# A two-layer decoder trunk on one core: which pairs of the second up projection run as seven products, and the order of work around them

## The chip, the core and the metric

One core of one Trainium2 chip. The metric is the device time of one execution in microseconds (us), median of several runs. The kernel before takes 1085.06 us (three runs, 1084.51 to 1085.06).

## The reference, cut to what matters

```python
def short_conv_mixer(h, w_in, conv_w, w_out):
    b_gate, c_gate, u = jnp.split(h @ w_in, 3, axis=-1)
    v = c_gate * u
    ...
    return (b_gate * conv) @ w_out

def squared_relu_mlp(h, w1, w2):
    return jnp.square(jax.nn.relu(h @ w1)) @ w2

def reference(x, ...):
    for layer in range(DEPTH):                       # 2 layers
        h = rms_norm(x, norm_mix[layer])
        if layer < N_A_LAYERS:                       # layer 0
            x = x + short_conv_mixer(h, ...)
        else:                                        # layer 1
            x = x + nsa_mixer(h, ..., shared, rel_bias)
        x = x + squared_relu_mlp(rms_norm(x, norm_mlp[layer]), mlp_w1[layer], mlp_w2[layer])
        if layer == N_A_LAYERS - 1:
            shared = nsa_shared_kv(rms_norm(x, kv_norm), w_kv, ...)
    return rms_norm(x, final_norm)
```

512 tokens, model width 1024, hidden width 4096, everything in float32.

## The kernel before, in words

**Arithmetic.** Each float32 operand is split into a high and a low float16 half (`whi`, `wlo` for a weight; `xs`, `rh` and `rl` for activations), and a product of two takes three matmuls: high by high, low by high, high by low. The halves of the weights are made on the chip: DMA brings a float32 piece (`wst`), ScalarE (ACT) writes the high half, VectorE (DVE) the low one. `next_piece` hands pieces out in a fixed list, `ahead` converts some pieces ahead of use.

**Seven products.** Many of the large products are done block-wise with seven products of half-size blocks in place of eight. The price is sums of blocks, of the weights (`W_SUMS`, four additions on VectorE for each half piece) and of the activations (`R_SUMS`), and a combination of the results.

**An MLP.** The hidden width is done in two halves. A half is an up projection (`mlp_up`: eight pairs of 128 hidden channels, p = 0 to 7) and a down projection (`mlp_down`: four pairs of output channels, always as seven products, summing over eight hidden chunks c = 0 to 7 into the seven halves of banks "aabb" or "ccde"). A plain pair of an up projection is 48 matmuls of 512 columns in two accumulators from `acc()`; a pair as seven products (`seven`, only in the second up projection, for the pairs in `UP7`) is 84 matmuls of 256 columns. For these, the block sums of x are computed during the first up projection, kept in DRAM (`kept`), and loaded back by two DMAs that GpSimd (POOL) issues, into the parts 5 to 7 of the hidden activations `rh` and `rl`: these parts must first have been read for the last time by the down projection. For the pairs in `MADE7` the sums and splits of the weights are done earlier in the kernel and kept in DRAM (`make_seven`), so that at use there are only loads.

**Stages, from the start:** the short convolution mixer of layer 0 with its output projection (four pairs), the MLP of layer 0 (up, down, up, down), the attention of layer 1 with its output projection, the MLP of layer 1, the final norm.

**What sets the order.** Accumulators of plain pairs turn through "aabbcc" (`acc`; the counter `turn[0]` is set to 1 at each up projection and otherwise runs on). The first mixer, the second up projection of each layer and the attention are each recorded as a plan: a list scheduler (`Plan.issue`) orders the recorded instructions of all engines by keys, and the tables in `SHIFTS`, one per plan, shift the keys of single instructions (before, only the fourth, for the second up projection of layer 1, has entries). What is outside a plan is ordered by the framework. In the profile a line 268 is an instruction of a plan, a line 302 one outside; after the change these lines are 342 and 376.

Of the kernel before, what the change touches and what calls it, by code (L numbers as in the profile page):

```python
# [10 lines left out]
F32 = mybir.dt.float32  # L11
# [27 lines left out]
def onehot_buckets():  # L39
# [5 lines left out]


SHIFTS = (
    (),
    (),
    (),  # L50
    (
# [15 lines left out]
    ),  # L67
)

# [238 lines left out]
def body(ctx, tc, x, rel_bias, norm_mix, norm_mlp, mlp_w1, mlp_w2, a_w_in, a_conv_w, a_w_out,  # L308
# [26 lines left out]
    def begin_plan(**late):  # L335
        banks.clear()
        turns.clear()
        plan.begin(*[u for i in sorted(ready) for u in ready[i]], *[staged[i] for i in sorted(staged)], **late)
# [23 lines left out]
    def seven_blocks(w, c0):  # L362
        v = w.rearrange("(c j p) n -> c p j n", j=2, p=128)
        for c in (0, 2):
            pieces.append(([v[c + k, :, :, c0:c0 + 256] for k in range(2)], None, SW))

    def down_blocks(w, p, half):

        v = w.rearrange("(j c p) n -> c p j n", j=2, p=128)
        for c in range(8 * half, 8 * half + 8, 2):  # L370
            pieces.append(([v[c + k, :, :, p * 256:(p + 1) * 256] for k in range(2)], None, SW2))

    def mlp_pieces(layer):
# [12 lines left out]


    SEVEN = [(2, 1), (2, 0), (3, 1), (3, 2), (3, 0)]
    UP7 = ((2, 3, 5), (1, 2, 3, 5))
    MADE7 = ((), (1,))  # L390
    FILL_AT, FILL = 4, 1
    made, made_out = {}, {}
    v = a_w_in[0].rearrange("(c p) (s n) -> c p s n", p=128, s=3)
# [385 lines left out]
        ACT.activation(dst[0], z[:, 4:8], AF.Copy)  # L779
        DVE.tensor_tensor(dst[1], z[:, 4:8], dst[0], op=OP.subtract)  # L780

    def seven(xs, sums, names, dlo, dhi=None):
        X_, W_, V_ = (bank(g)[:, 0:256] for g in "abc")
        ws = [next_piece(), next_piece()]
        cv = ahead()

        def block_of(hl, c, b):
            if b < 4:
                return xs[hl][:, 2 * c + b // 2, (b % 2) * 256:(b % 2) * 256 + 256]
            return sums[hl][:, 4 * c + b - 4]  # L790

        def product(i, ps, more=False):
            a, b = PRODUCTS[i]
            for c in range(4):
                wh, wl = (u[:, c % 2, a - 1] for u in ws[c // 2])
                xh, xl = (block_of(hl, c, b) for hl in range(2))
                PE.matmul(ps, wh, xh, start=c == 0 and not more, stop=False, skip_group_check=more)
                PE.matmul(ps, wl, xh, start=False, stop=False, skip_group_check=more)
                PE.matmul(ps, wh, xl, start=False, stop=c == 3, skip_group_check=more)

        u2, u5 = (wk[0].tile([128, 256], F32, name=n, bufs=1) for n in names)
        product(0, X_)
        ACT.activation(W_, X_, AF.Copy)
        product(4, V_)
        ACT.activation(u5, V_, AF.Copy)
        next(cv, None)
        product(2, W_, True)
        ACT.activation(u2, W_, AF.Copy)
        product(5, V_, True)
        DVE.tensor_tensor(dlo[:, 1], V_, u2, op=OP.add)  # L810
        next(cv, None)
        product(3, W_, True)
        DVE.tensor_tensor(dlo[:, 0], W_, u5, op=OP.add)
        product(1, X_, True)
        if dhi is not None:
            ACT.activation(dhi[:, 1], X_, AF.Copy)
        drain(cv)
        product(6, W_, True)
        if dhi is not None:
            ACT.activation(dhi[:, 0], W_, AF.Copy)  # L820
        return dlo, W_, X_
# [114 lines left out]
    for p in range(4):  # L936
        po = [acc(), acc()]
        pair(ys, po)
        if p < 3:
            drain(ahead())  # L940
        split_some(PACE_OUT[p])
        for m in range(2):
            residual_in(po[m], 2 * p + m, 1.0 / (SY * SW))
            ss.add(X[:, 2 * p + m])
        for m in range(2):
            split_gain(xs, 2 * p + m, X[:, 2 * p + m], "mlp0")
        drain(ahead())
# [8 lines left out]
    def mlp_up(xs, ss, rh, half, rb, gname, kept):  # L956
        turn[0], layer = 1, int(gname[-1])
        first = half == 0
        if not first:
            sums = [u[:, 5:8].rearrange("p a b n -> p (a b) n")[:, 0:16] for u in rh]  # L960
            for hl in range(2):
                POOL.dma_start(sums[hl], kept[:, hl])

        def rows():
            nonlocal rb
# [23 lines left out]
        for p in range(8):  # L989
            if not first and p in UP7[layer]:  # L990
                dlo = wk[0].tile([128, 2, 256], F32, name="dn_w", bufs=1)
                held[p] = seven(xs, sums, ("dn_p", "sv_u"), dlo)
                drain(ahead())
                squares(p)
                continue
            held[p] = [acc(), acc()]
            pair(xs, held[p], mid={ROOT_AT: ss.rstd} if first and p == 0 else {ROWS_AT: rows} if first and p == 1 else {})
            drain(ahead())
            if p or not first:
                squares(p)  # L1000
            if first and p in SUMS_AT:
                c = SUMS_AT.index(p)
                z = wk[0].tile([128, 8, 256], F32, name="ml_z", bufs=2)
                block_sums(c, gname, z, [u[:, 7, 0:4] for u in rh])
                for hl in range(2):
                    SPQ.dma_start(kept[:, hl, 4 * c:4 * c + 4], rh[hl][:, 7, 0:4])
# [34 lines left out]
    def mlp_down(rh, done, mid=None, last=None):  # L1041

        post = iter(())
        for p in range(4):
            bk = [bank(g) for g in ("aabb" if p % 2 == 0 else "ccde")]
            late = last and p == 3
            slot = {0: 0, 2: 2, 3: 4, 4: 6, 5: 1} if late else range(7)
# [3 lines left out]
            def product(i, c, w, terms=(0, 1, 2)):  # L1051

                a, b = PRODUCTS[i]
                wh, wl = (u[:, a - 1] for u in w)
                xh, xl = (u[:, c, b - 1] for u in rh)
                other = i == 5 if late else i % 2 == 1
                for n in terms:
                    PE.matmul(acc7[i], wl if n == 1 else wh, xl if n == 2 else xh, stop=c == 7 and n == 2,
                              start=c == 0 and n == 0 and not other, skip_group_check=other)

            some = (0, 2, 3, 4, 5) if late else range(7)
            ws = []
            for c in range(0, 4 if late else 8, 2):
                w = next_piece()
                for k in range(2):
                    for terms in ((0, 1), (2,)) if p == 0 and c + k == 7 else ((0, 1, 2),):
                        for i in some:
                            product(i, c + k, [u[:, k] for u in w], terms)
                    ws.append([u[:, k] for u in w])
                    behind = None  # L1070
                    if c + k == 0 and p:
                        behind = copied[0]
                    if c + k == 5 and mid and p:
                        behind = mid(p)
                    if k == (1 if c == 4 and mid else 0):
                        with tc.issue_after(behind.ins) if behind else nullcontext():
                            drain(ahead())
                    if c + k or not p:
                        next(post, None)
# [10 lines left out]
    def first_half(hp, xs, ss, gname):  # L1090
# [1 line left out]
        rh = tuple(hp.tile([128, 8, 7, 256], F16, name=n) for n in ("rh", "rl"))  # L1092
        rb = mlp_up(xs, ss, rh, 0, None, gname, kept)
        mlp_down(rh, None)
        begin_plan(DVE=3500.0, ACT=1000.0)
        mlp_up(xs, ss, rh, 1, rb, gname, kept)
        plan.issue()
        return rh
# [606 lines left out]
    xs = xm  # L1705
# [167 lines left out]
```

## Time and profile before

| | us |
|---|---|
| median of three runs | 1085.06 |
| the profiled execution | 1084.73 |
| its span, first to last instruction | 1082.9 |
| first mixer | 0 to 172.3 |
| layer 0: up, down, up, down | to 256.4, 329.8, 409.1, 482 |
| attention with output projection | to 763.5 |
| layer 1: up, down, up, down and final norm | to 847.6, 921, 999.1, 1082.9 |

The profile gives for each engine the busy time, and for each instruction its start, its length, and what ended the idle time before it. A start and a length in one row may stand for several equal instructions (x2, x7). Matmuls overlap, so their rate is read from one start to the next, not from the length of one. "PE" is TensorE; PEclk is its granted clock, 1.00 for 2.4 GHz.

### The profile page before, as it was taken

What the parts mean: (1) busy time and instruction counts of PE and PEld (TensorE: products, weight loads), DVE (VectorE), ACT (ScalarE), POOL (GpSimd) and SP (SyncE); (2) the same over time, 40 slices, a digit from 0 to 9 for tenths busy, and PEclk for the clock granted to TensorE, in tenths of its full rate; (3) what the DMA queues carried; (4) which work ended last, traced back from release to release, by engine and by line L of the source; (5) the groups of instructions that cost most, each with busy time, mean ns of one, the idle gap of its engine ahead of it and who ended that gap; (6) DMA issues with size and microseconds to landing.
All of it is one profiled execution on the core that took longest, in us unless ns stands there. A gap on an engine that the chain in (4) does not pass through costs nothing.

```text
span 1082.9 us, 21537 instructions
## 1 busy us (share of the span) xinstructions
PE 1072.7 (99%) x8442; PEld 737.6 (68%) x8442; DVE 953.3 (88%) x1824; ACT 619.8 (57%) x1010; POOL 64.9 (6%) x93
## 2 busy tenths in 40 slices
PE   9999999999999999999999999999999999999997
PEld 4457844446885768886766696675444788775897
DVE  7999987998985999989886789997899796899996
ACT  6665555666333654437766687865666532464453
POOL 2000000000000000000002022311000000000022
PEclk9999999999999999999999999999999999999999
DMA  8535788453432334306634262002753236521332
GB/s 278 170 105 176 233 270 254 149 162 126 129 112 103 115 119 137 100 20 178 198 111 124 78 196 80 21 21 60 215 155 125 71 117 188 173 79 59 104 113 79
DMA packets 160774, 143.48 MB, mean 133 GB/s; under 512 B 9388, under 2 KB 149376, under 8 KB 160160
## 3 DMA queue, kind: packets, MB, share of 16 engines
q1 hardware_dynamic: 157248, 132.61, 39.8%
q10 hardware_dynamic: 2464, 4.70, 1.4%
q0 software_dynamic: 960, 4.80, 1.2%
q8 instruction: 66, 1.08, 0.4%
q14 instruction: 36, 0.29, 0.1%
HBM read 123.55 MB, written 15.51 MB: 128 GB/s over the span
## 4 chain that ended last, share of the span: by engine, by line
PE 94%; DVE 3%; ACT 1%; issue 1%; POOL 0%; POOLq 0%; ACTq 0%; DVEq 0%
PE a L268 19%; PE b L268 16%; PE c L268 14%; PE c L302 13%; PE a L302 12%; PE b L302 12%; PE d L302 4%; PE d L268 3%; PE e L302 2%; DVE at_s L268 1%; PE e L268 1%; ACT xq L268 0%; DVE wlo L268 0%; DVE X L302 0%; DVE wst L268 0%
## 5 line engine op out<-in xcount | busy, mean ns | idle before, releaser
L302 PEld LDWEIGHTS <-whi 128*128 128x128 f16 x2272 | 222.3, 98 | 79.8
L268 PEld LDWEIGHTS <-whi 128*128 128x128 f16 x1824 | 175.6, 98 | 114.7 <-issue 1.6
L302 ACT ACTIVATE whi<-wst 128x1792 f16<-128x1792 f32 (+1 forms) x92 | 132.8, 1458 | 111.5 <-DVE wst L302 53.5
L302 DVE SCALAR_TENSOR_TENSOR wlo<-wst,whi 128x1792 f16<-128x1792 f32 (+1 forms) x92 | 158.0, 1724 | 5.3 <-ACT whi L302 5.3
L268 ACT ACTIVATE whi<-wst 128x896 f16<-128x896 f32 (+5 forms) x144 | 116.5, 843 | 70.3 <-DVE wst L268 19.1
L268 DVE SCALAR_TENSOR_TENSOR wlo<-wst,whi 128x896 f16<-128x896 f32 (+5 forms) x144 | 135.1, 964 | 9.9 <-ACT whi L268 9.6
L302 PEld LDWEIGHTS <-wlo 128*128 128x128 f16 x1136 | 111.1, 98 | 40.6
L268 PEld LDWEIGHTS <-wlo 128*128 128x128 f16 x912 | 89.2, 98 | 64.8 <-DVE wlo L268 0.9
L302 DVE TENSOR_TENSOR wst<-wst 128x256 f32<-128x256 f32 x232 | 89.5, 430 | 11.5 <-DMA wst<-mlp_w_dram 10.5
L268 ACT ACTIVATE at_p<-at_s,at_m 128x128 f32<-128x128 f32 (+3 forms) x128 | 71.0, 556 | 29.2 <-DVE at_m L268 26.8
L268 PE MATMUL a<-xs,whi 128*128 128x512 f16 (+2 forms) x368 | 85.6, 321 | 0.1
L268 DVE CUSTOM_DVE_ANT_0 at_s<-b,T 128x128 f32<-128x128 f32 (+3 forms) x128 | 59.2, 486 | 15.6 <-PE b L268 13.5
L302 PE MATMUL a<-rh,whi 128*128 128x256 f16 x256 | 69.1, 273 | 0.0
L302 PE MATMUL a<-rh,wlo 128*128 128x256 f16 x256 | 69.1, 273 | 0.0
L302 PE MATMUL a<-rl,whi 128*128 128x256 f16 x256 | 67.8, 273 | 0.0
L302 PE MATMUL c<-rh,whi 128*128 128x256 f16 x248 | 67.6, 273 | 0.0
L302 PE MATMUL c<-rh,wlo 128*128 128x256 f16 x248 | 67.6, 273 | 0.0
L302 PE MATMUL c<-rl,whi 128*128 128x256 f16 x248 | 67.6, 273 | 0.0
L268 ACT ACTIVATE at_ph<-c 128x512 f16<-128x512 f32 (+2 forms) x96 | 51.0, 533 | 20.2 <-PE c L268 17.7
L268 DVE SCALAR_TENSOR_TENSOR at_pl<-c,at_ph 128x512 f16<-128x512 f32 (+2 forms) x96 | 59.2, 618 | 2.5 <-ACT at_ph L268 2.2
L268 PE MATMUL b<-xs,whi 128*128 128x512 f16 (+1 forms) x248 | 60.2, 327 | 0.0
L268 PE MATMUL a<-xs,wlo 128*128 128x512 f16 (+2 forms) x184 | 58.4, 321 | 0.0
(314 smaller groups left out, 2490.6 us busy)
## 6 DMA issues: line engine op xcount, KB each, us to landing
wst<-mlp_w_dram SPq DMA_DIRECT2D x228, 256.0 KB, 3.6
early<-pre_hl SPq DMA_DIRECT2D x14, 512.0 KB, 3.6
wst<-mlp_w_dram SPq DMA_DIRECT2D x48, 128.0 KB, 2.7
wst<-a_w_in_dram SPq DMA_DIRECT2D x20, 256.0 KB, 3.8
wst<-w_kv_dram SPq DMA_DIRECT2D x10, 512.0 KB, 4.5
T<-ext_d ACTq DMA_DIRECT2D x4, 1056.0 KB, 5.8
wst<-a_w_in_dram SPq DMA_DIRECT2D x8, 512.0 KB, 4.7
wst<-a_w_out_dram SPq DMA_DIRECT2D x8, 512.0 KB, 4.0
```

The lines of the kernel that those rows point to most:

```text
L268: getattr(self.engines[t["e"]], t["op"])(*t["args"], **t["kw"])
L302: return real(*args, **kwargs)
```

## The change

- `UP7`: pair 0 of the second up projection becomes seven products in both layers; in layer 1 pair 1 becomes a plain pair. `seven` gets the banks for pair 0 as "aba" in place of "abc".
- `MADE7`: pair 2 of both layers has its sums and splits made early. In layer 0 that happens at the last pair of the first mixer's output projection, in layer 1 in the attention stage as before (there for pair 1).
- `LAST_FIRST`: the last pair of each first down projection reads the hidden chunks 4 to 7 first, then 0 to 3. The loads of x's block sums are issued ahead of the plan of the up projection.
- `SHIFTS`: tables for the first mixer (372 entries) and for both second up projections (one table of 115 entries for both, in place of the one of layer 1).

```diff
 SHIFTS = (
-    (),
-    (),
+    (
+        (8, -10837), (9, -9292.8), (10, -8766.4), (11, -8651.3), (12, -7709.2), (13, -8454.9), (14, -3982.6),
...
+    ),
+    (
+        (24, -791.7), (27, -2324), (50, 2128.2), (53, -278.2), (56, 1133.3), (58, 944.9), (59, 309.9), (61, -167),
...
+    ),
     (),
...
+    LAST_FIRST = ((0, 2, 4, 6), (4, 6, 0, 2))
+
     def down_blocks(w, p, half):
 
         v = w.rearrange("(j c p) n -> c p j n", j=2, p=128)
-        for c in range(8 * half, 8 * half + 8, 2):
+        for c in (8 * half + u for u in LAST_FIRST[not half and p == 3]):
...
-    UP7 = ((2, 3, 5), (1, 2, 3, 5))
-    MADE7 = ((), (1,))
+    UP7 = ((0, 2, 3, 5), (0, 2, 3, 5))
+    MADE7 = ((2,), (2,))
...
-    def seven(xs, sums, names, dlo, dhi=None):
-        X_, W_, V_ = (bank(g)[:, 0:256] for g in "abc")
+    def seven(xs, sums, names, dlo, dhi=None, groups="abc"):
+        X_, W_, V_ = (bank(g)[:, 0:256] for g in groups)
...
         split_some(PACE_OUT[p])
+        for j in MADE7[0] if p == 3 else ():
+            now = []
+
+            def raw_half():
+                now[:] = [wk[0].tile([128, PIECE], F32, name="pre_in", bufs=2)]
+                return now[0][:, 0:512]
+            drain(make_seven(0, j, raw_half, lambda: now[0][:, 512:PIECE], lambda: wk[0].tile(
+                [128, 2, PIECE], F16, name="pre_hl", bufs=2)[:, :, 0:896].rearrange("p i (b n) -> p i b n", n=128)))
...
-        if not first:
-            sums = [u[:, 5:8].rearrange("p a b n -> p (a b) n")[:, 0:16] for u in rh]
-            for hl in range(2):
-                POOL.dma_start(sums[hl], kept[:, hl])
+        sums = [u[:, 5:8].rearrange("p a b n -> p (a b) n")[:, 0:16] for u in rh]
...
-                held[p] = seven(xs, sums, ("dn_p", "sv_u"), dlo)
+                held[p] = seven(xs, sums, ("dn_p", "sv_u"), dlo, groups="abc" if p else "aba")
...
+            at = LAST_FIRST[done is None and p == 3]
...
-                    PE.matmul(acc7[i], wl if n == 1 else wh, xl if n == 2 else xh, stop=c == 7 and n == 2,
-                              start=c == 0 and n == 0 and not other, skip_group_check=other)
+                    PE.matmul(acc7[i], wl if n == 1 else wh, xl if n == 2 else xh, stop=c == at[3] + 1 and n == 2,
+                              start=c == at[0] and n == 0 and not other, skip_group_check=other)
...
-                            product(i, c + k, [u[:, k] for u in w], terms)
+                            product(i, at[c // 2] + k, [u[:, k] for u in w], terms)
...
-        begin_plan(DVE=3500.0, ACT=1000.0)
+        soon = 0 in UP7[int(gname[-1])]
+
+        def load_sums():
+            for hl in range(2):
+                POOL.dma_start(rh[hl][:, 5:8].rearrange("p a b n -> p (a b) n")[:, 0:16], kept[:, hl])
+        if soon:
+            load_sums()
+        begin_plan(DVE=7000.0 if soon else 3500.0, ACT=1000.0)
+        if not soon:
+            load_sums()
```

What this does to the order of instructions is shown at three places.

VectorE between the third and the last pair of the first down projection of layer 0 (`wst` are weights, summed in place; `X<-c` is the combination of the last pair). Before:

```order
L302 TENSOR_TENSOR X<-X,dn_w 128x2x256
L268 TENSOR_TENSOR wst_3322<-wst_3322 128x2x128 x4
L268 TENSOR_TENSOR wst_3327<-wst_3327 128x2x128 x3
L268 SCALAR_TENSOR_TENSOR wlo_3427<-wst_3322,whi_3426 128x896 x2
L302 SCALAR_TENSOR_TENSOR X<-c,X 128x256
```

Now:

```order
L376 TENSOR_TENSOR X<-X,dn_w 128x2x256
L376 TENSOR_TENSOR wst_3159<-wst_3159 128x2x128 x3
L376 TENSOR_TENSOR wst_3214<-wst_3214 128x2x128
L376 TENSOR_TENSOR wst_3159<-wst_3159 128x2x128
L376 TENSOR_TENSOR wst_3214<-wst_3214 128x2x128 x3
L342 TENSOR_TENSOR wst_3284<-wst_3284 128x2x128
L376 SCALAR_TENSOR_TENSOR wlo_3385<-wst_3159,whi_3384 128x1792
L376 SCALAR_TENSOR_TENSOR wlo_3443<-wst_3214,whi_3442 128x1792
L376 SCALAR_TENSOR_TENSOR X<-c,X 128x256
```

The sums and splits of pair 0's two pieces stand ahead of the end of the down projection, where before work of pair 2 stood.

VectorE at the lead-in of the attention (`KD` and `Q` are the first keys and queries, `rb` the row factors). Before:

```order
L268 TENSOR_TENSOR at_s_5164<-a,rb 128x512
L268 TENSOR_TENSOR at_s_5165<-a,rb 128x512
L268 SCALAR_TENSOR_TENSOR xq<-X,vec,xq 128x512
L268 TENSOR_TENSOR KD<-at_s_5164,KD 64x512 x2
...
L268 TENSOR_TENSOR at_s_5175<-b,rb 128x512
L268 TENSOR_TENSOR at_s_5164<-b,rb 128x512
L268 TENSOR_TENSOR sq<-sq,ssacc 128x128
L268 TENSOR_TENSOR Q_5174<-at_s_5175,Q_5174 64x512 x2
```

Now:

```order
L342 TENSOR_TENSOR at_s_5252<-c,rb 128x512
L342 TENSOR_TENSOR at_s_5253<-c,rb 128x512
L342 SCALAR_TENSOR_TENSOR xq<-X,vec,xq 128x512
L342 TENSOR_TENSOR KD<-at_s_5252,KD 64x512 x2
...
L342 TENSOR_TENSOR at_s_5263<-a,rb 128x512
L342 TENSOR_TENSOR at_s_5252<-a,rb 128x512
L342 TENSOR_TENSOR sq<-sq,ssacc 128x128
L342 TENSOR_TENSOR Q_5262<-at_s_5263,Q_5262 64x512 x2
```

The keys lie in bank c in place of a, the queries in a in place of b; the values that TensorE does after the queries are in a both times.

TensorE where the output projection of the attention (`big`) goes over into the first up projection of layer 1 (`xs`). Before:

```order
L268 MATMUL c<-big,whi 128x512
L268 LDWEIGHTS wlo
L268 MATMUL c<-big,wlo 128x512
L302 LDWEIGHTS whi
L302 MATMUL b<-xs,whi 128x512
```

Now:

```order
L342 MATMUL b_5275<-big_5326,wlo_5412 128x512
L376 LDWEIGHTS whi_9409
L376 MATMUL c_9456<-xs_5406,whi_9409 128x512
...
L376 MATMUL c_9457<-xs_5406,wlo_9410 128x512
L376 LDWEIGHTS whi_5417
L376 MATMUL b_9383<-xs_5406,whi_5417 128x512
```

The last output pair lies in bank b in place of c, and 12 matmuls of pair 1 (bank c) stand ahead of pair 0 (bank b).

## Rows read from the trace of the kernel before

**Rows 1.** Page, busy time, share of the span and instructions of TensorE:

```profile
PE 1072.7 (99%) x8442; PEld 737.6 (68%) x8442; DVE 953.3 (88%) x1824; ACT 619.8 (57%) x1010; POOL 64.9 (6%) x93
```

**Rows 2.** Busy time by stretch; the first line names the columns:

```profile
core 0: us, PE busy (x) PEld busy (x) DVE busy (x) ACT busy (x) POOL busy (x), PEclk, DMA share, GB/s
0.00:172.30 172.30, 170.92 (x1001) 99.03 (x1002) 154.68 (x248) 103.34 (x156) 5.86 (x13) 1.00 0.67 211
256.40:329.80 73.40, 73.40 (x674) 65.73 (x672) 60.64 (x99) 27.14 (x21) 0.00 (x0) 1.00 0.38 115
329.80:409.10 79.30, 79.30 (x495) 48.14 (x493) 71.28 (x119) 42.58 (x47) 1.14 (x2) 1.00 0.38 120
921.00:999.10 78.10, 78.10 (x530) 51.65 (x529) 72.36 (x120) 41.07 (x46) 1.06 (x2) 1.00 0.34 106
640.00:720.00 80.00, 77.91 (x952) 58.58 (x948) 76.54 (x234) 62.24 (x173) 18.69 (x26) 1.00 0.21 65
1062.00:1082.90 20.90, 14.64 (x180) 13.72 (x178) 11.61 (x29) 5.67 (x22) 5.77 (x8) 0.90 0.26 101
```

**Rows 3.** Timeline of POOL from 328; then the page's DMA issues (median to landing):

```profile
329.92 0.61 POOL L268 DMA_DIRECT2D rh<-kept_mlp  x1 [146.46 <-PE e L302]
330.55 0.53 POOL L268 DMA_DIRECT2D rl<-kept_mlp  x1
...
rh<-kept_mlp POOLq DMA_DIRECT2D x2, 1024.0 KB, 6.2
```

**Rows 4.** Timeline of DVE, 316 to 329 (start, length, idle before and its end):

```profile
316.36 2.68 DVE L268 TENSOR_TENSOR wst<-wst 128x256 f32<-128x256 f32 x7
319.05 2.09 DVE L268 SCALAR_TENSOR_TENSOR wlo<-wst,whi 128x896 f16<-128x896 f32 x2
328.68 0.42 DVE L302 SCALAR_TENSOR_TENSOR X<-c,X 128x256 f32<-128x256 f32 x1 [7.53 <-ACT dn_p L302]
```

**Rows 5.** Timelines of DVE, POOL and PE, 161 to 185:

```profile
161.35 0.69 DVE L268 SCALAR_TENSOR_TENSOR X<-a,X 128x512 f32<-128x512 f32 x1 [1.30 <-PE a L268]
...
169.35 1.23 DVE L268 SCALAR_TENSOR_TENSOR pre_hl<-pre_in,pre_hl 128x1024 f16<-128x1024 f32 x1 [1.44 <-ACT pre_hl L268]
...
178.41 1.22 DVE L302 SCALAR_TENSOR_TENSOR wlo<-wst,whi 128x1024 f16<-128x1024 f32 x1 [1.43 <-ACT whi L302]
182.21 0.16 DVE L302 TENSOR_SCALAR rs_a<-d 128x4 f32<-128x4 f32 x1 [2.57 <-PE d L302]
...
182.45 1.02 POOL L302 TENSOR_TENSOR rs_r<-rs_a,expo 128x4 f32<-128x4 f32 x1 [158.84 <-DVE rs_a L302]
...
184.62 0.60 PE L302 MATMUL e<-ident,rs_r 128*128 128x128 f32 x4
```

**Rows 6.** Timelines of DVE and PE at the attention's lead-in, 504 to 507:

```profile
504.32 0.28 DVE L268 TENSOR_TENSOR sq<-ssacc 128x128 f32<-128x128 f32 x1
504.52 1.28 DVE L268 TENSOR_TENSOR at_s<-b,rb 128x512 f32<-128x512 f32 x2
...
504.27 0.27 PE L268 MATMUL a<-whi,xs 128*128 128x256 f16 x1
...
506.77 0.29 PE L268 MATMUL b<-KD,Q 128*128 128x128 f16 x2 [0.37 <-DVE Q L268]
```

**Rows 7.** Timelines of DVE and PE where layer 1's first up projection begins:

```profile
763.02 1.22 DVE L302 SCALAR_TENSOR_TENSOR wlo<-wst,whi 128x1024 f16<-128x1024 f32 x1
...
766.02 1.28 DVE L268 SCALAR_TENSOR_TENSOR X<-c,X 128x512 f32<-128x512 f32 x2
...
763.74 0.38 PE L302 MATMUL b<-xs,wlo 128*128 128x512 f16 x1
```

**Rows 8.** Timeline of PE, 5 to 7, filling matmuls ahead of the first real one:

```profile
5.53 1.06 PE L268 MATMUL c<-idle 128*128 128x512 f16 x2
```

**Rows 9.** Timelines of PE and POOL behind the sum of squares, 773 to 775:

```profile
773.18 0.59 PE L302 MATMUL b<-xs,whi 128*128 128x512 f16 x2
...
773.60 1.17 POOL L302 TENSOR_TENSOR rs_r<-rs_a,expo 128x4 f32<-128x4 f32 x1 [26.82 <-DMA wst<-mlp_w_dram]
```

100 rows, old and new, of the table SHIFTS are left out of this document.

## Prediction

> **What bounds the kernel now.** I read the page's busy times first, then the busy time of each engine by stage, then the timelines of single engines around the seams between stages. TensorE is busy for 1072.7 us of 1082.9 [rows 1]. The stage table says where the missing 10 us of TensorE lie [rows 2]: in the four MLP stretches it has none (73.40 of 73.40, 79.30 of 79.30, 78.10 of 78.10). Some 1.4 us are in the first stage, 2.1 in 640 to 720, 6.3 in the last 21 us. So in the stretches that the change is about, the time is the number of matmul columns and nothing else; VectorE has 8 us of air in the second up projection of layer 0 and 5.7 in that of layer 1. Two things can move the total: fewer columns, or a wait of TensorE that is not there now. The reader should see that all idle time outside the end of the kernel is under 4 us, so that no rearrangement can win much more than the columns it saves. What a measurement of this kernel tells from no change is about 0.2%, 2.2 us.
>
> **Pair 0 as seven products.** The table has the price without any model: the second up projection of layer 0 is five plain pairs and three of seven products, 79.30 us; that of layer 1 is four and four, 78.10 us [rows 2]. One pair turned over is worth 1.20 us. The change brings layer 0 to four and four, so **-1.20 us**. Layer 1 has four before and after (pair 0 takes the place of pair 1): **0**.
>
> **The reload of x's block sums.** Now both loads are issued at 329.92 and 330.55, when the up projection has begun, and land 6.2 us after issue (median) [rows 3]. Pair 0 needs them at its second product, 12 matmuls in. A matmul of the down projection (256 columns) takes 73.40 / 672 = 0.109 us, so one of 512 columns (79.30 - 3 x 84 x 0.109) / 240 = 0.216 [rows 2]; the new order frees the blocks 88 matmuls, 9.6 us, before the end instead of 4. Issued at about 320.2 and 320.8 they land near 327; they are needed at 329.8 + 12 x 0.109 = 331.1. Slack about 4 us, cost 0. POOL has nothing else queued there. What is behind the loads on POOL is not due for tens of us.
>
> **Preparing pair 0.** Its two pieces need 8 additions on VectorE (2.68 / 7 = 0.38 us each) and two splits of 1792 columns, each as long as the 2.09 us that two of 896 take [rows 4]: 7.2 us, against 7.53 us in which VectorE stands idle before the end of that down projection [rows 4], where 2.68 + 2.09 us of plan work also give way. Walking it from 316.36, with ScalarE's conversions in between, the second piece is ready near 324.5, 5 us before it is due. Cost 0; without that gap those 7 us would fall into the up projection, which has 8 us of VectorE to spare.
>
> **Pair 2's sums kept in DRAM.** In the second up projection of layer 0 pair 2's sums and splits go, 8 x 0.38 + 4 x 1.045 = 7.2 us of VectorE, replaced by loads; TensorE doesn't wait there, so nothing is gained. The same work, cut smaller, moves ahead of the last output projection of the first mixer: 16 additions of 128 columns at 0.20 us (start to start, the second of [rows 6] after the first) and 8 splits at up to 0.64 us (half of the two-instruction row of [rows 7]) are at most 8.3 us; the lower bound is the 7.2 above. VectorE has there 1.30 + 1.44 + 1.43 + 2.57 = 6.7 us of idle time [rows 5], and the new order runs the two banks of the last two output pairs one after the other, so that the first is free for VectorE 24 x 0.216 = 5.2 us sooner. What is late next, if it does not fit, is the sum of squares: rs_a at 182.21, POOL's power until 183.47, the transposes at 184.62 [rows 5], 1.15 between the last two, of which I leave 0.15 for the handover: 1.0 us of slack. Bounds 0 and 8.3 - 6.7 - 1.0 = 0.6 us; I take 0, because of the bank that comes free sooner. In layer 1 the same work only changes its pair: 0.
>
> **The start.** The new table puts the copy of the gains ahead of the first weight conversion on ScalarE. The first real matmul follows two filling ones that take 1.06 us from 5.53 [rows 8]; it can't come sooner than by these. Bounds -1.1 and, for an order that is late by half as much, +0.5; I take **-0.3**, since the split of x's first block still stands in between.
>
> **Banks.** This is what the diff does not show. Two plain pairs fewer take four turns fewer of the rotating banks, and later stages inherit it. At the lead-in of the attention the first queries now lie in bank a, and the values that follow them go to the same bank. VectorE empties the first half of the queries from 504.52 [rows 6], 0.64 us, so the values, due at 504.27, begin at about 505.2: 0.95 late. Ahead of the first logits stand 15 of them instead of 18, and the logits already waited for Q: 18 from 504.27 end at 506.23, and they start at 506.77 [rows 6]. The logits come at 505.2 + 15 x 0.109 = 506.86, 0.09 later than now and with three matmuls fewer done: **+0.4 us**.
>
> At the seam from the attention to the first up projection of layer 1 the last output pair now lies in bank b, where pair 0 wants to begin. TensorE therefore takes 12 matmuls of pair 1 first. Their low weight half is made by VectorE from 763.02, 1.22 us; it is due with the third matmul, at 763.74: +0.55. After them (12 x 0.216 = 2.6 us) pair 0 begins at 766.45 and its bank is emptied from 766.02, 0.64 each [rows 7]: +0.25. Together **+0.8 us**, between 0 (VectorE ahead by as much) and 1.5 (a split more in front).
>
> Behind that, the transposes of the row factors come right after the last chunk, which starts at 773.18 and has 6 matmuls (to 774.48), while POOL's power ends at 773.60 + 1.17 = 774.77 [rows 9]; now more chunks stand in between. **+0.3**, between 0 and 0.5.
>
> **The sum.** -1.20 - 0.3 + 0.4 + 0.8 + 0.3 = 0.0. The profiled execution took 1084.73 us (span 1082.9 and 1.8 around it), 0.33 under the median of the runs, 1085.06. So 1084.7 beside the profiled one and 1085.0 beside the median; I give 1084.9.
>
> **The rivals.**
> *The savings stay and the bank waits don't count (0.22).* The two waits are each under 1 us and come from my walk of VectorE; if VectorE is ahead by that much there, -1.2 and up to -1.1 at the start, with up to 1 us of the first stage's 1.4, remain: 1081.7 to 1083.9 beside the median, about two thirds of it past the bound of 2.2. For it: the idle time that TensorE has in 640 to 720 (77.91 of 80.00) [rows 2] could swallow a lead-in that is late. Against it: VectorE is busy 76.54 of 80.00 there, so what is late for VectorE stays late.
>
> *VectorE is late at the end of the first mixer (slower, 0.07).* If none of the four gaps can be used, since each ends with a wait of its own, 8.3 us less the 1.0 of slack come out as a wait of TensorE for the row factors: +7.3, 1092. It is slower by over 0.2% from the point at which less than 8.3 - 1.0 - 2.2 = 5.1 us of the 6.7 are usable.
>
> *The reload comes late (slower, 0.04).* POOL's issue must get through while VectorE works through pair 0's sums and splits. Here two issues took 0.61 and 0.53 us beside VectorE's additions from PSUM and SBUF [rows 3]; if each had to wait out one split of 2.09 us [rows 4], they land 4.2 us later, near 331.2, just at the need. What is over costs in both layers: it decides from 5.2 us late (2 x 1.1), and 7 us late are 2 x 2.9 = +5.8, 1090.7. The Trainium skill has a rule that speaks for it: in SBUF — State Buffer, section Who interferes with whom, a VectorE instruction in a two-port mode locks GpSimd out and so holds up the descriptors of a load issued there. The trace of this stretch has only instructions with two tensor inputs on VectorE [rows 4], and shows no such hold.
>
> *Waits lower TensorE's clock (slower, 0.02).* With waits of some 0.5 us in a row, as at the new seams, the clock could fall from 2.4 to 1.2 GHz, and 5 us of work after it would take 10: 1090. In 640 to 720, where TensorE loses 2.1 us in many small waits, the granted clock is 1.00; it is lower only at the end (0.90 from 1062 on) [rows 2]. TensorE: Matmul & The Clock Gate of the Trainium skill, section A second HAM failure mode: psum-queue depth-cycling, says that short idle times between groups that turn through the banks make the clock swing; the stretch from 640 to 720 does not agree.
>
> *The change does nothing to the count* can be excluded: the program has 48 matmuls of 512 columns less and 84 of 256 more.
>
> **How the numbers follow.** My own case, within about 1.5 us of 1084.9, has 0.65. The four rivals take 0.35; 0.08 of the first stays within the bound. The range goes from within the first rival, 1082.4, to my case with the upper bound of every term (-1.2 + 0.5 + 0.6 + 0.4 + 1.5 + 0.5 = +2.3) on the median: 1087.4. Faster by over 0.2%: 0.14, the rest of the first rival; within it 0.65 + 0.08 = 0.73; slower 0.07 + 0.04 + 0.02 = 0.13.
>
> **What would show it.** The second up projection of layer 0 in 78.1 us with TensorE busy throughout; both reloads issued about 9 us before it; TensorE's gap before the values near 504, and one near 763 before the third matmul of bank c. Wrong it would be if TensorE idles over 1 us before product 2 of pair 0, at the transposes near 184, or if the clock falls below 1.00 before 1060.

## The result, and the profile after

The changed kernel takes 1091.01 us (1090.69 to 1091.43, four runs) against 1084.88 for the kernel before beside it; the ratio is 1.0057, 95% interval 1.0042 to 1.0071. It is slower by 6.1 us, and outside the range that was given. Its profiled execution has a span of 1089.2 us.

The seams between the stages, read from the starts of TensorE's matmuls in both traces, say where the time went:

| stretch | before, us | after, us | difference |
|---|---|---|---|
| start to the first up projection | 172.16 | 172.64 | +0.48 |
| layer 0: up and down | 157.48 | 157.48 | 0 |
| layer 0: second up | 79.31 | 83.37 | +4.06 |
| layer 0: second down | 73.36 | 73.98 | +0.62 |
| attention with output projection | 281.00 | 281.09 | +0.09 |
| layer 1: first up | 84.12 | 85.16 | +1.04 |
| layer 1: down, second up, rest | 235.5 | 235.5 | 0 |

First the page's busy line of the changed kernel, which answers to [rows 1]:

```profile
PE 1073.9 (99%) x8478; PEld 741.6 (68%) x8478; DVE 955.7 (88%) x1845; ACT 622.4 (57%) x1015; POOL 62.8 (6%) x93
```

TensorE is busy 1.2 us longer although it has 1.2 us of work less; the window view (columns as in [rows 2]) shows where most of this lies: the second up projection of layer 0, where the work is less, is busy for 79.80 us in place of 79.30.

```profile
172.60:330.00 157.40, 157.40 (x1068) 104.60 (x1067) 137.62 (x225) 80.33 (x74) 2.16 (x3) 1.00 0.49 151
330.00:332.50 2.50, 0.40 (x4) 0.11 (x2) 2.22 (x2) 0.00 (x0) 0.00 (x0) 1.00 0.00 1
332.50:335.00 2.50, 1.20 (x8) 0.79 (x9) 2.50 (x4) 0.00 (x0) 0.00 (x0) 0.87 0.22 64
335.00:337.70 2.70, 2.70 (x15) 1.92 (x13) 2.70 (x8) 1.33 (x2) 0.00 (x0) 0.50 0.83 205
330.30:413.50 83.20, 79.80 (x529) 52.26 (x528) 75.82 (x125) 43.86 (x49) 0.00 (x0) 0.98 0.43 130
927.00:1005.00 78.00, 78.00 (x531) 51.65 (x528) 71.05 (x120) 41.95 (x47) 0.00 (x0) 1.00 0.37 112
```

From 172.6 to 330 nothing is lost. Then TensorE does 1.6 us of work in 5.0, and for 2.7 us after that it is busy all the time at a granted clock of 0.50, the 1.2 GHz level. The same up projection in layer 1 runs without a gap. TensorE's timeline names the wait:

```profile
330.13 0.27 PE L342 MATMUL a<-xs,whi 128*128 128x256 f16 x1
332.69 0.28 PE L342 MATMUL a<-xs,wlo 128*128 128x256 f16 x1 [2.30 <-DVE wlo L376]
...
334.63 0.39 PE L342 MATMUL a<-xs,wlo 128*128 128x256 f16 x1 [1.11 <-DVE wlo L376]
```

It waits for the low weight halves of pair 0's two pieces. In VectorE's timeline these stand behind an addition that waits for a DMA:

```profile
320.67 2.76 DVE L376 TENSOR_TENSOR wst<-wst 128x256 f32<-128x256 f32 x8
330.28 0.42 DVE L342 TENSOR_TENSOR wst<-wst 128x256 f32<-128x256 f32 x1 [6.85 <-DMA wst<-mlp_w_dram]
330.62 3.95 DVE L376 SCALAR_TENSOR_TENSOR wlo<-wst,whi 128x1792 f16<-128x1792 f32 x2
334.49 0.41 DVE L376 SCALAR_TENSOR_TENSOR X<-c,X 128x256 f32<-128x256 f32 x1
```

The x8 are pair 0's own sums, done at 323.4. The next one, of plan lines (342), belongs to the third weight piece, which pair 0 does not need. Its four loads of 128 KB are issued by SP (SyncE, which issues the weight loads) from 320.17 to 323.54, and in the middle of them POOL issues the reload of x's sums, 2 MB (timelines of SP and POOL, then the DMA issues from 322 on with their time to landing):

```profile
320.17 3.37 SPq L376 DMA_DIRECT2D wst<-mlp_w_dram  x4
...
321.24 0.61 POOL L376 DMA_DIRECT2D rh<-kept_mlp  x1 [136.43 <-PE e L376]
321.87 0.54 POOL L376 DMA_DIRECT2D rl<-kept_mlp  x1
...
rl<-kept_mlp POOLq DMA_DIRECT2D x1, 1024.0 KB, 8.5
wst<-mlp_w_dram SPq DMA_DIRECT2D x2, 128.0 KB, 8.6
```

The last two small loads land with the big one, 8.6 us after issue; such loads took 2.7 us in the kernel before by the page's median. DMA: Bandwidth & Descriptors of the Trainium skill, section Issuing engines are not separate DMA queues, says that loads of all issuing engines run on the same 16 engines and interleave; the trace agrees.

In layer 1 the changed kernel does the same without a collision. SP, POOL and VectorE there:

```profile
913.06 2.50 SPq L376 DMA_DIRECT2D wst<-mlp_w_dram  x4
...
918.18 0.53 POOL L376 DMA_DIRECT2D rh<-kept_mlp  x1 [133.80 <-PE e L376]
...
917.06 0.42 DVE L342 TENSOR_TENSOR wst<-wst 128x256 f32<-128x256 f32 x1 [0.74 <-DMA wst<-mlp_w_dram]
```

The four loads are out 2.6 us before the reload, the addition waits 0.74 us, and TensorE loses nothing.

The smaller losses are waits of TensorE at the seams where the banks have turned. Its timeline shows them at the second down projection (bank b), at the values, at the first matmul with pair 1's low half, and at the row factors:

```profile
416.09 0.27 PE L376 MATMUL b<-rh,whi 128*128 128x256 f16 x1 [0.46 <-DVE ml_t L342]
...
510.43 0.28 PE L342 MATMUL a<-whi,xs 128*128 128x256 f16 x1 [0.82 <-DVE at_s L342]
...
769.34 0.39 PE L376 MATMUL c<-xs,wlo 128*128 128x512 f16 x1 [0.17 <-DVE wlo L376]
...
783.32 0.54 PE L376 MATMUL e<-ident,rs_r 128*128 128x128 f32 x3 [0.19 <-POOL rs_r L376]
```

### The profile page after: what moved, and what is told of

It reads as the page before. It is cut to its first block, busy times and chain, and to the rows that moved or that the text cites. A ratio compares the mean times of both kernels' runs of the same rounds, so it can differ in the third digit from the quotient of the medians.

```text
span 1089.2 us, 21667 instructions
## 1 busy us (share of the span) xinstructions
PE 1073.9 (99%) x8478; PEld 741.6 (68%) x8478; DVE 955.7 (88%) x1845; ACT 622.4 (57%) x1015; POOL 62.8 (6%) x93
## 4 chain that ended last, share of the span: by engine, by line
PE 72%; DVE 17%; DMA 4%; ACT 3%; issue 2%; SPq 0%; POOL 0%; DVEq 0%; ACTq 0%; POOLq 0%
PE a L342 17%; PE b L342 13%; PE c L342 10%; PE c L376 8%; PE b L376 8%; PE a L376 8%; DMA wst<-mlp_w_dram 4%; DVE wlo L376 4%; PE d L376 3%; PE d L342 3%; DVE wlo L342 2%; DVE wst L376 2%; PE e L376 2%; DVE rl L342 1%; DVE rl L376 1%
## 5 line engine op out<-in xcount | busy, mean ns | idle before, releaser
L376 ACT ACTIVATE whi<-wst 128x1792 f16<-128x1792 f32 (+1 forms) x92 | 135.0, 1486 | 128.4 <-DVE wst L376 56.4
L376 DVE SCALAR_TENSOR_TENSOR wlo<-wst,whi 128x1792 f16<-128x1792 f32 (+1 forms) x92 | 160.4, 1755 | 8.8 <-ACT whi L376 8.8
L342 ACT ACTIVATE whi<-wst 128x896 f16<-128x896 f32 (+5 forms) x138 | 112.4, 842 | 67.2 <-PE b L342 35.5
L342 DVE SCALAR_TENSOR_TENSOR wlo<-wst,whi 128x1024 f16<-128x1024 f32 (+5 forms) x138 | 129.0, 959 | 8.6 <-ACT whi L342 8.4
L376 DVE TENSOR_TENSOR wst<-wst 128x256 f32<-128x256 f32 x248 | 93.9, 423 | 16.9 <-DMA wst<-mlp_w_dram 16.1
L342 PE MATMUL a<-xs,whi 128*128 128x512 f16 (+2 forms) x368 | 82.7, 313 | 0.1
```

Of the source, the lines that this page charges most:

```text
L342: getattr(self.engines[t["e"]], t["op"])(*t["args"], **t["kw"])
L376: return real(*args, **kwargs)
```

## The experiments

Theory: the early reload of x's sums meets the loads of the next weight piece, and since one addition on that piece stands in VectorE's queue ahead of pair 0's splits, all of the delay reaches TensorE. Rivals: pair 0's preparation is too much work for the time; or the reload itself is late.

**The reload left out in layer 0** (so four of that layer's pairs multiply stale values).

```diff
-        if soon:
+        if soon and gname != "mlp0":
             load_sums()
```

> The changed kernel without the two loads of x's block sums in layer 0 (pairs 0, 2, 3 and 5 of that layer multiply stale values). Theory: these 2 MB fill the DMA engines from 321 on and hold up the last 128 KB of the next weight piece; VectorE's first addition on that piece stands ahead of the two splits of pair 0, so it waits 6.85 us and TensorE with it (2.46 and 1.27 us, then 1.4 us at half clock). Then without the loads the wait of VectorE near 323 falls under 1 us, both waits and the half clock go, and the span is 1089.2 - 5.1 = 1084.1. Rival: pair 0's additions and splits are too much for VectorE and ScalarE before the end of the down projection whatever DMA does; then the waits stay and the span is 1089.2.

Measured: 1085.97 us (one run), span 1084.2, and no wait of TensorE at the start of that up projection. VectorE's addition:

```profile
325.35 0.42 DVE L342 TENSOR_TENSOR wst<-wst 128x256 f32<-128x256 f32 x1 [1.55 <-DMA wst<-mlp_w_dram]
```

It still waits 1.55 us, and not under 1 as expected, but no longer 6.85. The work on VectorE and ScalarE is the same, so pair 0's preparation is not too much; the 2 MB are the cause.

**One addition moved in VectorE's order.**

```diff
         self.active = False
+        dve = [n for n in order if tasks[n]["e"] == "DVE"][:3]
+        if [tasks[n]["op"] for n in dve[1:]] == ["tensor_tensor"] * 2:
+            order.remove(dve[1])
+            order.insert(order.index(dve[2]) + 1, dve[1])
```

> The changed kernel with one addition on VectorE moved in each second up projection: the first of the third weight piece now behind the first combination of pair 0, no longer ahead of the splits of pair 0. The loads stay as they are. Theory: the piece still lands at 330, but nobody waits for it; splits from 324.3 to 328.3, no wait of TensorE at the start of the up projection of layer 0, 1091.0 - 5.1 = 1085.9, slower than before by 1.0 (the start, the turned banks, a wait at the second down projection). Rival, that the collision itself delays pair 0's own pieces or the sums: a wait of over 1 us stays at the start and the time is over 1087.

Measured: 1086.80 us (1085.81 to 1087.74, ten runs), ratio 1.0019 (1.0009 to 1.0029). VectorE's timeline in that kernel:

```profile
321.92 2.77 DVE L380 TENSOR_TENSOR wst<-wst 128x256 f32<-128x256 f32 x8
325.57 3.96 DVE L380 SCALAR_TENSOR_TENSOR wlo<-wst,whi 128x1792 f16<-128x1792 f32 x2 [0.88 <-ACT whi L380]
330.20 0.42 DVE L380 SCALAR_TENSOR_TENSOR X<-c,X 128x256 f32<-128x256 f32 x1 [0.67 <-ACT dn_p L380]
```

The loads still meet (SP's four are issued beside the reload), but nobody is behind the addition, and TensorE is busy without a gap; the up projection takes 78.31 us. So it takes both: the collision and the order. The median is 0.9 us over the expected one. In the profiled execution (1087.08) the first up projection begins at 173.68, 1.0 us later than in the changed kernel, with 0.84 us of idle time before x's transposes at 11.64; the other executions were not profiled.

**The first table of shifts emptied** (so the first mixer has the old order, with pair 2's sums in it).

```diff
 SHIFTS = (
-    (
...
-    ),
+    (),
```

> The changed kernel with the first table of shifts empty, as before the change. Layer 0's first up projection began at 172.64 with the table and at 172.16 in the kernel before. If the table itself loses that half microsecond (a wait of 0.7 us for the second block of x at 6.9), it begins near 172.2 and the total is 1090.5. If the table was there to make room for pair 2's sums in the first mixer, without it VectorE is late for the row factors of the up projection: a wait of up to 3 us near 185 and 1091 to 1093.

Measured: 1084.43 us (1083.76 to 1085.65, eight runs), ratio 0.9997 (0.9987 to 1.0007). This was a surprise: not 0.5 but 6.6 us come back. In its trace, SP, POOL and VectorE:

```profile
318.31 2.50 SPq L322 DMA_DIRECT2D wst<-mlp_w_dram  x4
...
320.97 0.61 POOL L322 DMA_DIRECT2D rh<-kept_mlp  x1 [136.58 <-DVE wst L322]
...
322.24 0.43 DVE L288 TENSOR_TENSOR wst<-wst 128x256 f32<-128x256 f32 x1 [0.68 <-DMA wst<-mlp_w_dram]
322.59 3.95 DVE L322 SCALAR_TENSOR_TENSOR wlo<-wst,whi 128x1792 f16<-128x1792 f32 x2
```

All four loads are out 0.2 us before the reload, and the addition waits 0.68 us in place of 6.85. The window of the second up projection of layer 0 is then the one that was forecast:

```profile
329.87:408.01 78.14, 78.14 (x531) 51.69 (x529) 71.40 (x122) 43.96 (x49) 0.00 (x0) 1.00 0.44 133
```

What the table does is seen at the split that frees the weight buffer, with the table and without:

```profile
318.13 2.02 DVE L376 SCALAR_TENSOR_TENSOR wlo<-wst,whi 128x1792 f16<-128x1792 f32 x1
...
316.27 2.02 DVE L322 SCALAR_TENSOR_TENSOR wlo<-wst,whi 128x1792 f16<-128x1792 f32 x1
```

The loads into that buffer wait for that split. TensorE, which releases the reload, is only 0.3 us later with the table. The two orders differ on VectorE from the mixer through the first up projection. From 11 us into the down projection on the order is the same, and there VectorE is later with the table by 1.0 to 1.6 us, counted from the begin of the first up projection, and by 1.6 at this split. Which instruction makes these 1.6 us was not followed further.

**VectorE made later without the table**, to test that it is only a question of who comes first.

```diff
-                DVE.scalar_tensor_tensor(lo[:, k], b[:, k, 1:], sc, hi[:, k], op0=OP.mult, op1=OP.subtract)
+                for _ in range(2 if i == twice[0] else 1):
+                    DVE.scalar_tensor_tensor(lo[:, k], b[:, k, 1:], sc, hi[:, k], op0=OP.mult, op1=OP.subtract)
```

(`twice[0]` is the last weight piece of layer 0's first down projection.)

> The changed kernel with an empty first table (span 1082.9), in which VectorE does one split of layer 0's first down projection twice, the one that sets the weight buffer free for the next load (its second result is the same). That is 2.6 us more for VectorE, which stands idle for longer than that before the end of the down projection. Theory: it is only a question of who comes first. The loads of the next piece, issued from 318.45 to 320.34, move to about 321.0 to 322.9, behind the first load of x's sums at 321.1; the last of them lands near 331, VectorE waits some 6 us in front of pair 0's splits, TensorE loses 5 to 6 us, span 1088 to 1089. Rival, that the table cost its time elsewhere and the late load is only a sign of it: the 2.6 us vanish in VectorE's idle time, span 1082.9 to 1083.5.

Measured: 1092.63 us (one run), span 1090.9. SP and VectorE:

```profile
320.88 2.51 SPq L322 DMA_DIRECT2D wst<-mlp_w_dram  x4
...
331.05 0.42 DVE L288 TENSOR_TENSOR wst<-wst 128x256 f32<-128x256 f32 x1 [7.55 <-DMA wst<-mlp_w_dram]
```

The second split is 2.0 us of work for VectorE, which had that time to spare. It moves the loads back by 2.6 us and costs 8.0 us of span: the same wait as in the changed kernel, without its table. 7.0 us of it lie in that up projection (85.10 us in place of 78.12), more than the 5 to 6 expected, and 0.7 at the start of the execution.

**The old time of the reload, without the table**: last pair in the old order, loads behind the begin of the plan.

```diff
-    LAST_FIRST = ((0, 2, 4, 6), (4, 6, 0, 2))
+    LAST_FIRST = ((0, 2, 4, 6), (0, 2, 4, 6))
...
-        if soon:
-            load_sums()
...
-        if not soon:
-            load_sums()
+        load_sums()
```

> The changed kernel with an empty first table, the last pair of the first down projection again in the old order and the loads of x's sums behind the begin of the plan, as before the change; pair 0 still as seven products. My own working: the loads are issued some 0.5 us before the end of the down projection, land 6 to 7 us later, 5 us after the second product needs them; 5 us in each layer, and some 1.4 us each of half clock behind so long a wait: 1084.4 + 13 = 1097. Rival, that pair 0's own pieces or the order of the plan hide it: under 1088.

Measured: 1116.37 us (one run), span 1114.6. TensorE:

```profile
338.73 0.37 PE L288 MATMUL a<-rh,whi 128*128 128x256 f16 x1 [5.66 <-DMA rh<-kept_mlp]
```

The wait for the sums is the one expected (3.69 us in layer 1), but seven more waits of 0.3 to 2.3 us follow it in each second up projection, so that 32 us go and not 13. That the order of the plan was made for a pair 0 in time is the likely reason; no run tests it. Pair 0 needs the early reload; what the runs above find wrong with it is only its meeting with the other loads.

**The banks**, alone in the kernel before, taken back in the changed kernel, and taken back together with the table (the counter is set where each kernel's second up projection of layer 0 ends; 9 is the change's value, 11 that of before).

```diff
         mlp_up(xs, ss, rh, 1, rb, gname, kept)
+        if gname == "mlp0":
+            turn[0] = 9
         plan.issue()
```

> The kernel before with nothing changed but the counter of accumulators, set to 9 after layer 0's second up projection, where the change leaves it. Theory: waits of 0.98 us before the values, 0.3 us each at two places and 0.35 before the row factors appear as in the changed kernel: 1084.7 + 1.5 = 1086.2. Rival: the banks cost only where other things of the change are late too; then 1084.7.

Measured: 1086.06 us (1085.63 to 1088.07, ten runs), ratio 1.0013 (1.0003 to 1.0022). By the seams the attention is 0.37 longer and the first up projection of layer 1 takes 85.16 in place of 84.12: the same +1.04 as in the changed kernel.

> The changed kernel with the counter of the accumulators set to 11 after layer 0's second up projection, as it stood there before the change, so that attention and the next seams use their old banks. Theory: the wait of 0.98 us before the values near 509 goes back to 0.54 before the logits, and the three waits of 0.33, 0.30 and 0.35 us near 769, 771 and 783 go: 1091.0 - 1.0 = 1090.0 (the lead-in's part was already given back within the attention). Rival, that these small waits only take the place of others: 1091.0 and the same waits elsewhere.

Measured: 1088.64 us (three runs), ratio 1.0040 (1.0024 to 1.0056). More comes back than expected. The seam waits near 769 to 783 are gone and the idle time before the logits is 0.37 us again, as in [rows 6], while the long wait near 330 stays (2.63 and 0.61 us idle). By the seams of the two profiled executions 0.36 us come back in the attention and 1.04 in the up projection behind it; the other 0.9 lie in stages that the counter does not reach, 0.37 of them in layer 0's second up projection.

> The changed kernel with an empty first table and the counter of accumulators put back to 11. Theory: the two costs are separate places and add up. Table empty gave 1084.4; the banks alone gave 2.4 us in the changed kernel, of which 1.0 to 1.4 lie at the seam of the attention and the up projection and 0.4 at the lead-in: 1084.4 - 1.5 = 1082.9, faster than before by 1.8 (0.17%). Rival, that the banks' gain was in part a different start in that run: 1083.5 to 1084.

Measured: 1083.25 us (1082.37 to 1083.75, eleven runs), ratio 0.9985 (0.9976 to 0.9994), between the time expected and its rival. With both taken out, the change is a gain of 1.7 us, and this kernel beats both.

**All seams mended, the table kept**: the addition moved and the counter at 11.

> The changed kernel with its first table, with the addition of the third piece moved behind pair 0's first combination and the counter put back to 11: all that cost time at the seams taken out, the table kept. Theory that the table costs only by the collision at the seam: 1083.2, as with the table empty and the banks put back. Rival, that the table also costs at the start of the kernel (the waits for x's second block, 0.6 to 0.8 us near 7, in each run with it): 1084 to 1085.5.

Measured: 1084.54 us (1084.0 to 1086.36, eleven runs), ratio 0.9997 (0.9988 to 1.0006). This is the rival's time, 1.3 us over the run without the table (the kernel before takes 1084.57 beside this run and 1084.92 beside that one). Not all of that is the table: each second up projection takes 78.31 us in place of 78.12, as in the run above with the moved addition. The profiled execution, the fastest of this kernel, begins the first up projection 0.3 us later than that of the run without the table. So the table seems to cost something besides the collision; where, stays open, since the slower executions were not profiled.

**Another start of the counter**, to get pair 7 out of bank b.

```diff
-        turn[0], layer = 1, int(gname[-1])
         first = half == 0
+        turn[0], layer = 1 if first else 3, int(gname[-1])
```

> The changed kernel with an empty first table, in which the counter of accumulators starts at 3 in place of 1 in both second up projections. It then ends at 11, as before the change, so the attention gets its old banks, and pair 7 lies in bank c, not b. Theory: beside the gain of the banks (1084.4 - 1.2) the wait at the begin of layer 0's second down projection (0.46 us idle behind the emptying of bank b in the changed kernel) goes too: 1082.7. Rival: the scheduler now puts the second half of pair 6, which is in b, last, so the same wait comes from there: 1083.2 to 1084.

Measured: 1094.41 us (1093.58 to 1099.07, four runs), ratio 1.0101. Both times were missed: waits of 1.90 and 1.4 us appear within each second up projection (82.6 us in place of 78.12). Other banks give the plan another order, for which its table of shifts was not made; that this is the reason is not tested. The wait at bank b in the second down projection is still there (0.47 us idle), as the rival had it, but with the plan upset the run does not settle what pair 7 does.

## Why the prediction was wrong

**The step that failed** is the one on preparing pair 0: "Walking it from 316.36, with ScalarE's conversions in between, the second piece is ready near 324.5, 5 us before it is due. Cost 0". The amount of work was right (2.76 and 3.95 us against 7.2). Two things were left out. VectorE's order, which was shown ahead of the prediction, has an addition of the third piece between the sums and the splits; the walk counted it as ready. And that piece's loads were never priced. The reload was asked only what it waits for and who waits for it, not which other loads it would now run beside; moved 9 us ahead, it met the piece that stood in the queue before the due work. Waits of 2.30 and 1.11 us and half a clock came of it: 83.37 us in place of 78.12, +5.25. The walk also began too early: pair 0's sums start at 320.67, not at 316.36, and in the run with the empty table, where almost nothing holds them up, the second split ends at 322.59 + 3.95 = 326.54, 3.3 us before it is due and not 5.

**The reload itself** was on time: issued at 321.24 and 321.87, in 0.61 and 0.54 us as before, with no hold by VectorE. Its slack was mis-sized, though: the second half landed 8.5 us after issue, at 330.4 and not near 327, so it was some 1 us ahead of 330.13 + 12 x 0.109 = 331.4, when pair 0 would have needed it, and not 4. The rival that priced a late reload looked at the wrong transfer.

**One pair as seven products, -1.20**: right. Without the collision that stretch takes 78.12 us against 79.31.

**The clock.** The rival with the half clock had 0.02 and was argued away by the small waits of 640 to 720. Behind two long waits close together it came: some 15 matmuls at double time, 1.5 of the 5.25 us. It did not come at the seams with waits of 0.2 to 0.8 us.

**The banks**: the mechanism and the sizes were right. +0.8 and +0.3 at the seam were 1.04 together. The lead-in's +0.4 (0.82 us idle before the values) is 0.37 in the kernel before with the turned banks, and 0.36 and 0.42 come back in the attention when the banks are put back in the changed kernel, with the table and without. That the attention of the changed kernel as a whole is only 0.09 longer has another cause: it is 0.3 us shorter than before also with the banks put back; why, stays open. The second down projection (+0.62, TensorE waits at bank b for VectorE) was not forecast. The bank alone does not make that wait: the run with the empty table has the same banks up to there and takes 73.36, as before, while the run with the empty table and the counter put back, which is the same kernel up to there, takes 73.99; VectorE empties the bank 0.7 us later in it, counted from the begin of that down projection.

**The start**: -0.3 was forecast, +0.48 measured in one execution. The start scatters by more than that: the first up projection begins between 172.30 and 173.68 in the five profiled executions with the table, between 172.00 and 173.10 in the five of the changed kernel without it. What the traces do show is that the gain is not there: the two filling matmuls start at 5.58, against 5.53 before, and TensorE then waits 0.56 us for x's second block (at 7.78), which the copy of the gains does not bring. Four of the five executions with the table have such a wait near 7.8, none without it.

**Pair 2's sums in the first mixer**: nothing lost at the row factors, with the table or without, as forecast.

## What to carry to other kernels

When a transfer is moved ahead, list what else is on the DMA engines at its new time, and for each load that it delays, who stands behind its first reader in that engine's queue. A cover of several microseconds on the engine does not help if one instruction in front of the due work waits for something else. Where two transfers are released by different engines, a shift of 2 us on one of them decides between nothing and the whole length of the larger transfer, so issue the small urgent one first or keep its reader behind the due work.

## What was not expected of the hardware

A load of 128 KB issued beside 2 MB from another issuing engine took 8.6 us, as long as the 1 MB load next to it (8.5), and not its own 2.7 and a share. And TensorE's granted clock was 0.50 over the 2.7 us from 335.0, after waits of 2.30 and 1.11 us within 4.5 us, though it had been busy without a gap for 157 us before.
